# Merged runs of divided-array matmuls in a hybrid attention step: sample projections, scores and value products

## The chip, the cores and the metric

The kernel runs on one core of a Trainium2 chip. The metric is the device time of one execution in microseconds (us), taken over several runs; lower is better. The profile is of one further execution of the same program.

## The reference, cut to what matters

One layer of a streaming encoder is computed for two inputs at once: a prompt of 512 tokens and a "sample" of 32 new tokens (T = 32) that attends to caches. Three head groups work side by side: A (band attention, 6 heads), B (attention to keys picked by an indexer, 6 heads) and M (attention to 256 memory rows, 4 heads). All heads have 64 columns, and all arithmetic is float32.

```python
def _band_sample(q, k_new, v_new, k_cache, v_cache, table):      # group A, sample
    k = jnp.concatenate([k_cache, k_new], axis=1)                # 512 + 32 keys
    v = jnp.concatenate([v_cache, v_new], axis=1)
    return _attend(q, k, v, bias)                                # softmax(q k^T / 8 + bias) v
...
def _dsa_sample(q, k_new, v_new, qi, ki_new, wi, k_cache, v_cache, ki_cache):   # group B, sample
    k = jnp.concatenate([k_cache, k_new], axis=1)                # 1024 + 32 keys
    v = jnp.concatenate([v_cache, v_new], axis=1)
    return _gather_attend(q, k, v, _indexer_scores(qi, ki, wi), topk)
...
om = _attend(qm, cache_mem_k[l], cache_mem_v[l], None)           # group M, sample: 256 keys, none new
```

The sample's q, k and v come from the same input projection `rmsnorm(x) @ w_in` as the prompt's.

## The kernel before

**Layout.** TensorE does matmuls on 128 rows (the contraction) by 128 columns (the stationary operand's width). The weights `raw` arrive in chunks by DMA; each chunk is split into a high part `wh` (on ACT) and a low part `wl` (on POOL, a few on DVE), and the prompt's projections use three full-array matmuls for each product. These matmuls are the main stream that fills TensorE from start to end.

**Divided arrays.** The sample has only 32 rows, so its matmuls use a part of the array: the call names a `tile_position`, and several such matmuls run side by side. In the trace the form of a matmul begins with rows by columns: `128*128` is the whole array, `128*32` four column strips, `64*32` eight tiles, `128*64` two column halves, `32*64` a quarter of the rows by half of the columns. A float32 matmul has two records in the trace. A run is a stretch of consecutive matmuls of one division.

**Who orders the work.** There is no loop nest over the whole. Every piece of work is a Python generator, and the class `Line` (line 45) keeps one estimated clock for each engine while the program is written out. A generator yields the time at which it wants to go on; `Line.beside` (line 198) lets it go on when TensorE's estimated clock has got there, and between two such points the main stream goes on. So the order on every engine is fixed when the program is built, by the estimated costs of `Line.cost` (line 63), which know nothing of a change of division. On the chip every engine works through its own list in that order and waits where an operand is late. `Line.room(k)` (line 299, inside the kernel) waits until k of TensorE's 8 PSUM banks are free.

**What the change touches.**
- `w_sample` (line 456) makes the sample's rows of six projections in this order: `i`, `ka`, `va`, `kb`, `qb`, `vb`. Each has four weight chunks `raw` of two 128-row blocks; the eight blocks go to four column strips, twice four matmuls, in two halves (line 462): the first half as soon as two chunks are there, the second when the other two are. `met` (line 411) tells `w_load` (line 414) which chunks are used up; a chunk's successor four places on is loaded only then.
- `sample_rows` (line 471) adds up the four strips on ACT and DVE into a tile of 32 rows (`kaS`, `vaS`, `kbS`, `qbS`, `vbS`), and scales it; it is then in `news`, and `store_new` writes it out.
- `sample` (line 1127) is the sample's attention for one group. It takes the heads four at a time (then the last two): for chunks of 512 keys, `room()`, a bank, and one matmul for each head (lines 1155 to 1162), each chunk with a reduction on DVE; then the softmax; then transposes to `pt` (lines 1184 to 1200); then the value products, two heads at a time (line 1203), with a `yield line.soon()` between the pairs. The block of new keys has w = 32 rows, so its matmuls use `vv[0:w]` and `pt[0:w]`: 32 rows of the array.

Of the kernel before, what the change touches and what calls it, by code (L numbers as in the profile page):

```python
# [9 lines left out]
F32 = mybir.dt.float32  # L10
# [7 lines left out]
P = 128  # L18
S = 512
T = 32  # L20
# [249 lines left out]
def hybrid_step(ctx: ExitStack, tc: tile.TileContext, a: dict):  # L270
    ctx.enter_context(tc.manual_schedule())
    nc = tc.nc
    line = Line()
# [15 lines left out]
    def bank():  # L289
        b = min(free_banks, key=lambda b: pp.free(f"b{b}"))  # L290
        free_banks.remove(b)
        t = pp.tile([P, 512], F32, tag=f"b{b}", name="bank")
        held[t.tensor.name] = b
        return t
# [4 lines left out]
    def room(k=1):  # L299

        yield from line.wait(lambda: len(free_banks) >= k)
        while True:
            t = sorted(pp.free(f"b{b}") for b in free_banks)[k - 1] + 0.4
            if t <= line.now():
                return
            yield t
            yield from line.wait(lambda: len(free_banks) >= k)
# [60 lines left out]
    def store_new(dst, nm):  # L368
        def when():
            yield from line.wait(lambda: nm in news)  # L370
            yield line.at(news[nm])
            DMA.dma_start(dst, news[nm])

        line.spawn(when())

# [79 lines left out]

    def w_sample():
        for nm, i, n in parties:
            yield from line.wait(lambda: len(raws) > i + 1 and x_done[0] > 1)
            yield line.sure(xF[:, 0:4, :], raws[i + 1])
            yield from room()  # L460
            p = bank()
            for j in (0, 2):
                yield from line.wait(lambda: len(raws) > i + j + 1 and x_done[0] > j + 1)
                yield line.sure(raws[i + j], raws[i + j + 1], xF[:, 2 * j:2 * j + 4, :])
                for q in range(4):
                    PE.matmul(p[q * T:(q + 1) * T, 0:n], xF[:, 2 * j + q, :], raws[i + j + q // 2][:, q % 2, :],
                              start=(j == 0), stop=(j == 2), tile_position=(0, q * T))
                met.extend((i + j, i + j + 1))
            line.spawn(sample_rows(nm, n, p))

    def sample_rows(nm, n, p):
        yield line.at(p)
        if nm in ("kb", "vb"):
            yield from line.wait(lambda: 0 in over)
        out = (cp.tile([T, 384], F32, tag={"kb": "kaS", "vb": "vaS"}.get(nm, nm + "S"), name=nm + "S") if nm != "i"
               else ix.tile([T, n], F32, name="zS"))
        A.copy(out, p[0:T, 0:n])
        for q in range(1, 4):
            yield line.at(out) - 0.2
            V.tensor_tensor(out, p[q * T:(q + 1) * T, 0:n], out, op=ALU.add)  # L480
        give(p)
        yield from line.wait(lambda: NT in normed)
        yield max(line.at(rs[0:T, NT:NT + 1]), line.at(out) - 0.2)
        V.tensor_scalar(out, out, rs[0:T, NT:NT + 1], None, op0=ALU.mult)
        news[nm] = out
        if nm in ("kb", "qb"):
            rope(out.rearrange("p (h d) -> p h d", d=64), out, T, 6, 64, ctab["cos64S"], ctab["sin64S"], V)

# [638 lines left out]
    def sample(mix, nh, nb, kt, cv, qT, kn, vn, pts, zin):  # L1127

        kt0 = (0, 3, 6)[mix]
        nn = nb * P
        nk = nn + (T if kn is not None else 0)
        if kn is not None:
            yield line.sure(kn)
            yield from room()
            p = bank()
            for hp, k in enumerate(kt):
                PE.transpose(p[:, hp * T:(hp + 1) * T], kn[:, hp * P:(hp + 1) * P], ident[:T, :T])
            for hp, k in enumerate(kt):  # L1140
                either(k[:, nn:nk], p[:, hp * T:(hp + 1) * T])
            give(p)
        yield line.sure(qT, *kt)
        yield from room(3)
        o_ps = bank()
        for g0 in range(0, nh, 4):
            hs = list(range(g0, min(g0 + 4, nh)))
            rows = T * len(hs)
            z = zin(g0, rows)
            yield line.at(z)  # L1150
            if mix == 0:
                V.tensor_scalar(z[0:rows], z[0:rows], -1.0, None, op0=ALU.mult)
            st = cp.tile([P, 8], F32, tag="stS", name="stS", bufs=2)
            np_ = 0
            for k0 in range(0, nk, 512):
                n = min(512, nk - k0)
                yield from room()
                sc = bank()
                for j, h in enumerate(hs):
                    r = 64 * (h % 2)  # L1160
                    PE.matmul(sc[T * j:T * j + T, 0:n], qT[r:r + 64, h // 2, -T:], kt[h // 2][r:r + 64, k0:k0 + n], start=True, stop=True,
                              tile_position=(r, T * j))
                if mix != 2:
                    V.tensor_tensor_reduce(z[0:rows, k0:k0 + n], in0=sc[0:rows, 0:n], in1=z[0:rows, k0:k0 + n],
                                           scale=1.0, scalar=3e38, op0=ALU.add,
                                           op1=ALU.min, accum_out=st[0:rows, np_:np_ + 1])
                    src = z
                    give(sc)
                else:
                    V.tensor_reduce(st[0:rows, 0:1], sc[0:rows, 0:n], axis=AX.X, op=ALU.min)  # L1170
                    src = sc
                np_ += 1
            V.tensor_reduce(st[0:rows, 4:5], st[0:rows, 0:np_], axis=AX.X, op=ALU.min)
            yield line.at(st)
            A.activation(z[0:rows, 0:nk], src[0:rows, 0:nk], AF.Exp, scale=-1.0, bias=st[0:rows, 4:5],
                         accum_out=st[0:rows, 5:6])
            if mix == 2:
                give(sc)
            yield line.at(st)
            V.reciprocal(st[0:rows, 6:7], st[0:rows, 5:6])  # L1180
            V.tensor_scalar(z[0:rows, 0:nk], z[0:rows, 0:nk], st[0:rows, 6:7], None, op0=ALU.mult)
            yield line.sure(z)
            blocks = []
            for k0 in range(0, nk, 512):
                yield from room()
                bw = []
                p = bank()
                for i, b in enumerate(range(k0, min(k0 + 512, nk), P)):
                    w = min(P, nk - b)
                    PE.transpose(p[0:w, i * rows:(i + 1) * rows], z[0:rows, b:b + w], ident[0:rows, 0:rows])  # L1190
                    bw.append((b // P, i, w))
                pt = pts[k0 // 512]
                full = sum(1 for x in bw if x[2] == P)
                if full:
                    either(pt[:, 0:full * rows], p[:, 0:full * rows])
                else:
                    w = bw[-1][2]
                    either(pt[0:w, 0:rows], p[0:w, 0:rows])
                give(p)
                blocks += [(pt, b, i, w) for b, i, w in bw]  # L1200
            yield line.sure(*(x[0] for x in blocks))
            yield line.sure(*cv)
            for j0 in range(0, len(hs), 2):
                for pt, b, i, w in blocks:
                    for j in (j0, j0 + 1):
                        h = hs[j]
                        e = h % 2
                        vv = cv[b // 4][:, b % 4, h * 64:h * 64 + 64] if b < nb else vn[:, h * 64:h * 64 + 64]
                        PE.matmul(o_ps[64 * e:64 * e + 64, (h // 2) * T:(h // 2 + 1) * T], vv[0:w],
                                  pt[0:w, i * rows + T * j:i * rows + T * j + T], start=(b == 0),  # L1210
                                  stop=(b * P + w == nk), tile_position=(0, 64 * e))
                yield line.soon()
        yield from line.wait(lambda: mix in gated)
        m = nh // 2
        o = cp.tile([P, 3 * T], F32, tag="oSt", name="oSt")
        yield line.at(gates[mix], o_ps) - 0.2
        ov = o[:, 0:m * T].rearrange("p (m c) -> p m c", m=m)
        V.scalar_tensor_tensor(ov, o_ps[:, 0:m * T].rearrange("p (m c) -> p m c", m=m), 0.5, gates[mix][:, :, S:N],
                               op0=ALU.mult, op1=ALU.mult)
        give(o_ps)  # L1220
        rounded(oS[:, kt0:kt0 + m, 0:T], ov)
        tsub(V, oS[:, kt0:kt0 + m, T:2 * T], ov, f(oS)[:, kt0:kt0 + m, 0:T])
        over[mix] = True
# [481 lines left out]
```

## Time and profile before

| | us |
|---|---|
| median of 3 runs | 382.3 |
| lowest and highest | 382.24, 385.92 |
| the profiled execution's own time | 382.36 |
| its span in the profile | 380.6 |
| TensorE (PE) busy | 360.6 (95%) |
| VectorE (DVE) busy | 282.9 (74%) |
| ScalarE (ACT) busy | 221.4 (58%) |
| GpSimd (POOL) busy | 181.8 (48%) |

Busy time of PE counts overlapping matmuls once and takes in the pipeline's fill, so a busy PE may still lose time between two matmuls; the start times of successive matmuls show it. By line, nearly everything is at L240, the helper that records each call, so the rows are told apart by the names of the tiles.

### The profile page before, as it was taken

The numbers are of one execution on the slowest core, as the hardware profiler recorded it, in microseconds if no ns is written. First come the engines' busy times: TensorE is split into PE (matmuls) and PEld (weight loads), VectorE is DVE, ScalarE is ACT, GpSimd is POOL, SyncE is SP. The second block draws the span as 40 slices with busy tenths as digits, with TensorE's granted clock in tenths as the row PEclk, the third lists the DMA queues.
The fourth block names the chain that finished last, engine by engine and source line by source line (L and its number), as shares of the span: only waits on it lengthen the run. The fifth ranks groups of instructions, "written<-read, shape, count | busy, mean of one in ns | idle before, by whom it ended". The sixth has DMA issues, their size and how long they took to land.

```text
span 380.6 us, 7964 instructions
## 1 busy us (share of the span) xinstructions
PE 360.6 (95%) x2959; PEld 322.7 (85%) x2959; DVE 282.9 (74%) x732; ACT 221.4 (58%) x519; POOL 181.8 (48%) x196
## 2 busy tenths in 40 slices
PE   7999899999999999999999989699999999999992
PEld 6889798989988978888887877588999879799992
DVE  2671887699999998899899989784975667452553
ACT  4854756897546758679655145437873656211353
POOL 1778951475442653327454737445135315133542
PEclk9999989999999999999999999899999999999997
DMA  7996441266474151322121211412236942120005
GB/s 242 363 355 214 118 140 55 96 187 167 138 244 119 29 155 31 89 63 84 52 75 42 84 47 69 128 29 63 68 126 213 368 153 88 40 98 2 0 16 220
DMA packets 41478, 46.35 MB, mean 122 GB/s; under 512 B 5184, under 2 KB 36544, under 8 KB 41440
## 3 DMA queue, kind: packets, MB, share of 16 engines
q1 hardware_dynamic: 41440, 45.85, 38.0%
q8 instruction: 23, 0.38, 0.4%
q14 instruction: 15, 0.12, 0.1%
HBM read 39.67 MB, written 6.16 MB: 120 GB/s over the span
## 4 chain that ended last, share of the span: by engine, by line
PE 67%; DVE 21%; ACT 4%; issue 3%; POOL 2%; DMA 2%; SPq 1%; POOLq 0%; DVEq 0%; ACTq 0%
PE bank L240 67%; DVE ysel L240 5%; DVE m L240 2%; DVE rt L240 2%; DMA raw<-in_w_in_dram 2%; DVE qbS L240 2%; DVE rank L240 1%; POOL wl L240 1%; DVE st L240 1%; DVE kbS L240 1%; ACT sq L240 1%; ACT wh L240 1%; DVE junkS L240 1%; POOL ss L240 1%; ACT junkS L240 1%
## 5 line engine op out<-in xcount | busy, mean ns | idle before, releaser
L240 POOL TENSOR_TENSOR wl<-raw,wh 128x512 fp32r<-128x512 f32 (+2 forms) x68 | 107.4, 1587 | 112.7 <-ACT wh L240 109.4
L240 PE MATMUL bank<-wh,xTh 128*128 128x384 f32 (+1 forms) x192 | 67.6, 352 | 3.0 <-DVE kb L240 1.6
L240 ACT ACTIVATE wh<-raw 128x512 fp32r<-128x512 f32 (+2 forms) x70 | 49.6, 715 | 28.3 <-PE bank L240 12.7
L240 PE MATMUL bank<-wl,xTh 128*128 128x384 f32 (+1 forms) x192 | 64.3, 336 | 0.9 <-POOL wl L240 0.6
L240 PE MATMUL bank<-wh,xTl 128*128 128x384 f32 (+1 forms) x192 | 64.2, 334 | 0.0
L240 ACT ACTIVATE z<-z,st 128x256 f32<-128x256 f32 (+3 forms) x70 | 38.0, 557 | 27.0 <-DVE st L240 26.8
L240 PE MATMUL bank<-xTh,wh 128*128 128x272 f32 x208 | 46.4, 304 | 0.0
L240 PEld LDWEIGHTS bank<-wh,xTh 128*128 128x128 f32 x192 | 37.0, 193 | 9.4 <-issue 6.8
L240 PE MATMUL bank<-xTh,wl 128*128 128x272 f32 x208 | 43.0, 288 | 0.0
L240 PE MATMUL bank<-xTl,wh 128*128 128x272 f32 x208 | 42.9, 288 | 0.0
L240 PEld LDWEIGHTS bank<-wl,xTh 128*128 128x128 f32 x192 | 36.8, 192 | 1.4 <-POOL wl L240 0.8
L240 PEld LDWEIGHTS bank<-wh,xTl 128*128 128x128 f32 x192 | 37.0, 193 | 0.3 <-DVE xTl L240 0.3
L240 PEld LDWEIGHTS bank<-xTh,wh 128*128 128x128 f32 x208 | 32.7, 189 | 4.7 <-issue 3.3
L240 PEld LDWEIGHTS bank<-xTl,wh 128*128 128x128 f32 x208 | 32.6, 188 | 0.0
L240 PEld LDWEIGHTS bank<-xTh,wl 128*128 128x128 f32 x208 | 32.6, 189 | 0.0
L240 DVE MAX8 m<-ysel 128x8 f32<-128x256 f32 (+2 forms) x48 | 26.4, 549 | 0.1
L240 DVE MATCH_REPLACE8 ysel<-m,ysel 128x256 f32<-128x256 f32 (+2 forms) x48 | 26.1, 543 | 0.0
L240 PE MATMUL bank<-ident,z 128*128 128x128 f32 (+1 forms) x161 | 25.2, 275 | 0.6 <-ACT tg L240 0.6
L240 DVE TENSOR_TENSOR xr<-bank,xr 128x256 f32<-128x256 f32 (+1 forms) x24 | 12.3, 511 | 15.8 <-PE bank L240 15.8
L240 DVE SCALAR_TENSOR_TENSOR ysel<-r,wI,ysel 128x256 f32<-128x256 f32 (+2 forms) x21 | 18.9, 898 | 4.5 <-ACT r L240 3.7
L240 PEld LDWEIGHTS bank<-ident,z 128*128 128x128 f32 (+1 forms) x161 | 18.0, 140 | 4.5 <-issue 0.9
L240 ACT ACTIVATE junkS<-ysS,bi_neg 128x1056 int8<-128x1056 f32 x16 | 18.7, 1171 | 3.5 <-DVE bi_neg L240 3.5
(313 smaller groups left out, 887.2 us busy)
## 6 DMA issues: line engine op xcount, KB each, us to landing
raw<-in_w_in_dram SPq DMA_DIRECT2D x20, 384.0 KB, 3.4
raw<-in_w_in_dram SPq DMA_DIRECT2D x26, 256.0 KB, 3.0
raw<-in_w_out_dram SPq DMA_DIRECT2D x8, 384.0 KB, 3.0
nat<-in_x_prompt_dram SPq DMA_DIRECT2D x4, 512.0 KB, 8.4
raw<-in_w_mem_kv_dram SPq DMA_DIRECT2D x8, 256.0 KB, 2.8
xr<-in_x_prompt_dram SPq DMA_DIRECT2D x4, 512.0 KB, 7.0
out_dram<-xr SPq DMA_DIRECT2D x4, 512.0 KB, 2.6
xr<-in_x_t_dram SPq DMA_DIRECT2D x3, 544.0 KB, 6.0
```

Source lines behind the costliest of these rows:

```text
L240: return fn(*args, **kw)
```

## The change

The first half of a projection no longer starts ahead: `w_sample` waits for all four chunks and then issues the eight matmuls together. The value tiles of the new keys get 128 rows, 96 of them set to zero on POOL, and so does the transposed block of new keys in `pt`; the value products use all 128 rows. The score chunks of four heads get their banks together and their matmuls are issued together, the reductions after them. The `yield` between pairs of heads is gone.

```diff
@@ store_new
-            DMA.dma_start(dst, news[nm])
+            DMA.dma_start(dst, news[nm][0:T])
@@ w_sample
-            yield from line.wait(lambda: len(raws) > i + 1 and x_done[0] > 1)
-            yield line.sure(xF[:, 0:4, :], raws[i + 1])
+            yield from line.wait(lambda: len(raws) > i + 3 and x_done[0] > 3)
+            yield line.sure(xF, *raws[i:i + 4])
             yield from room()
             p = bank()
             for j in (0, 2):
-                yield from line.wait(lambda: len(raws) > i + j + 1 and x_done[0] > j + 1)
-                yield line.sure(raws[i + j], raws[i + j + 1], xF[:, 2 * j:2 * j + 4, :])
                 for q in range(4):
                     PE.matmul(p[q * T:(q + 1) * T, 0:n], xF[:, 2 * j + q, :], raws[i + j + q // 2][:, q % 2, :],
                               start=(j == 0), stop=(j == 2), tile_position=(0, q * T))
-                met.extend((i + j, i + j + 1))
+            met.extend(range(i, i + 4))
@@ sample_rows
-        out = (cp.tile([T, 384], F32, tag={"kb": "kaS", "vb": "vaS"}.get(nm, nm + "S"), name=nm + "S") if nm != "i"
-               else ix.tile([T, n], F32, name="zS"))
+        full = (cp.tile([P, 384], F32, tag={"kb": "kaS", "vb": "vaS"}.get(nm, nm + "S"), name=nm + "S") if nm != "i"
+                else ix.tile([P, n], F32, name="zS"))
+        out = full[0:T]
+        if nm[0] == "v":
+            G.memset(full[T:2 * T], 0.0)
+            G.memset(full[2 * T:P], 0.0)
...
-        news[nm] = out
+        news[nm] = full if nm[0] == "v" else out
@@ sample, scores
-            for k0 in range(0, nk, 512):
-                n = min(512, nk - k0)
-                yield from room()
-                sc = bank()
+            cuts = [(k0, min(512, nk - k0)) for k0 in range(0, nk, 512)]
+            yield from room(len(cuts))
+            scs = [bank() for _ in cuts]
+            for sc, (k0, n) in zip(scs, cuts):
                 for j, h in enumerate(hs):
                     r = 64 * (h % 2)
                     PE.matmul(sc[T * j:T * j + T, 0:n], ...)
+            for sc, (k0, n) in zip(scs, cuts):
                 if mix != 2:
                     V.tensor_tensor_reduce(...)
@@ sample, transposed block of the new keys
-                    w = bw[-1][2]
-                    either(pt[0:w, 0:rows], p[0:w, 0:rows])
+                    G.memset(pt[T:2 * T, 0:rows], 0.0)
+                    G.memset(pt[2 * T:P, 0:rows], 0.0)
+                    either(pt[0:T, 0:rows], p[0:T, 0:rows])
@@ sample, value products
-                        PE.matmul(o_ps[...], vv[0:w],
-                                  pt[0:w, i * rows + T * j:i * rows + T * j + T], start=(b == 0),
+                        PE.matmul(o_ps[...], vv,
+                                  pt[:, i * rows + T * j:i * rows + T * j + T], start=(b == 0),
                                   stop=(b * P + w == nk), tile_position=(0, 64 * e))
-                yield line.soon()
```

## Rows read from the trace of the kernel before

**Rows 1.** Busy time by stretch: start:end, length, engines, PE clock, DMA
```profile
135.00:182.00 47.00, 47.00 (x458) 39.90 (x455) 42.26 (x143) 34.61 (x92) 20.74 (x23) 1.00 0.29 85
187.00:244.00 57.00, 50.22 (x368) 43.29 (x365) 52.84 (x111) 25.58 (x66) 32.81 (x26) 0.99 0.26 76
243.20:246.70 3.50, 3.06 (x11) 3.06 (x12) 2.25 (x8) 3.47 (x12) 0.81 (x1) 0.51 0.01 2
244.00:367.00 123.00, 123.00 (x1100) 111.78 (x1100) 73.86 (x207) 61.85 (x153) 47.89 (x39) 0.99 0.29 97
```

**Rows 2.** The chain that ended last, in order: start us, length us, engine
```profile
111.40 74.47 PE bank L240 x694
```

**Rows 3.** DVE in order of time: start us, us; in brackets idle before, releaser
```profile
148.27 0.69 DVE L240 CUSTOM_DVE_ANT_0 z<-bank,nb 128x512 f32<-128x512 f32 x1 [0.92 <-PE bank L240]
...
156.06 0.42 DVE L240 COPY tmpA<-bank 128x256 f32<-128x256 f32 x1 [1.11 <-PE bank L240]
...
182.30 0.69 DVE L240 COPY pt<-bank 128x512 f32<-128x512 f32 x1 [0.82 <-PE bank L240]
```

**Rows 4.** PE in order of time around the sample's projection runs (`raw,xF`)
```profile
19.30 0.51 PE L240 MATMUL bank<-raw,xF 128*32 128x384 f32 x4
19.63 0.51 PE L240 MATMUL bank<-raw,xF 128*32 128x384 f32 x4
...
35.89 0.85 PE L240 MATMUL bank<-raw,xF 128*32 128x384 f32 x8
36.67 0.45 PE L240 MATMUL bank<-wh,xTh 128*128 128x384 f32 x1
36.96 0.34 PE L240 MATMUL bank<-wh,xTl 128*128 128x384 f32 x1
37.13 0.34 PE L240 MATMUL bank<-wl,xTh 128*128 128x384 f32 x1
```

**Rows 5.** DMA issues from 13.5 to 14.2 us: count, KB, us to landing
```profile
raw<-in_w_in_dram SPq DMA_DIRECT2D x1, 384.0 KB, 6.2
```

**Rows 6.** PE in order of time in value products, groups A and B
```profile
135.07 0.66 PE L240 MATMUL bank<-tmpA,cache 128*64 128x32 f32 x16
135.66 0.30 PE L240 MATMUL bank<-tmpA,vaS 32*64 32x32 f32 x4
135.90 0.52 PE L240 MATMUL bank<-xTh,wh 128*128 128x272 f32 x2
...
320.74 1.12 PE L240 MATMUL bank<-ptS,cache 128*64 128x32 f32 x32
```

**Rows 7.** PE in order of time around a score run of group A
```profile
142.97 0.41 PE L240 MATMUL bank<-xTl,wh 128*128 128x272 f32 x2
143.22 0.41 PE L240 MATMUL bank<-xTh,wl 128*128 128x272 f32 x2
143.56 0.25 PE L240 MATMUL bank<-keysA,queried 64*32 64x32 f32 x4
143.74 0.52 PE L240 MATMUL bank<-xTh,wh 128*128 128x272 f32 x2
144.10 0.29 PE L240 MATMUL bank<-xTl,wh 128*128 128x272 f32 x1
```

**Rows 8.** POOL groups by form: shape, count, busy us, mean ns
```profile
L240 POOL MEMSET nb<- 64x128 f32 x3 | 0.6, 198 | 8.1 <-DVE nb L240 8.1
```

**Rows 9.** POOL in order of time: start us, us
```profile
135.34 2.54 POOL L240 TENSOR_TENSOR wl<-raw,wh 128x512 fp32r<-128x512 f32 x2
...
235.11 5.84 POOL L240 TENSOR_TENSOR wl<-raw,wh 128x768 fp32r<-128x768 f32 x3
```

**Rows 10.** DVE groups by form: the same operation on two sample tiles
```profile
L240 DVE TENSOR_TENSOR qbS<-qbS,cos64S 32x384 f32<-32x384 f32 x1 | 2.1, 2062 | 0.0
...
L240 DVE TENSOR_TENSOR kbS<-kbS,cos64S 32x384 f32<-32x384 f32 x1 | 0.5, 547 | 0.0
```

**Rows 11.** PE in order of time: its longest wait
```profile
243.64 0.19 PE L240 MATMUL bank<-bf_ok,over 128*128 128x1 bf16 x1 [3.60 <-DVE o L240]
```

More of the change, by code (lines that the diff above doesn't have):

```diff
@@ L1208, in sample @@
                         vv = cv[b // 4][:, b % 4, h * 64:h * 64 + 64] if b < nb else vn[:, h * 64:h * 64 + 64]
-                        PE.matmul(o_ps[64 * e:64 * e + 64, (h // 2) * T:(h // 2 + 1) * T], vv[0:w],
-                                  pt[0:w, i * rows + T * j:i * rows + T * j + T], start=(b == 0),
+                        PE.matmul(o_ps[64 * e:64 * e + 64, (h // 2) * T:(h // 2 + 1) * T], vv,
+                                  pt[:, i * rows + T * j:i * rows + T * j + T], start=(b == 0),
                                   stop=(b * P + w == nk), tile_position=(0, 64 * e))
-                yield line.soon()
         yield from line.wait(lambda: mix in gated)
```

## The prediction, made before the result was seen

> **What bounds the kernel now.** I read the busy time by stretch first. Between 135 and 182 us TensorE (PE) is busy all 47.00 us, between 187 and 244 us only 50.22 of 57, and from 244 to 367 us again all of it [rows 1]. Busy does not mean dense, so the second look is at the chain of work that ended last: it lies on PE from 111.40 us for 74.47 us, that is to 185.9 [rows 2]. The reader is to see three regimes in these rows: PE sets the pace to about 186 us; from 187 to 244 us DVE does (52.84 of 57 us busy); after 244 us nothing holds PE up any more.
>
> The third look is at DVE in order of time. Ahead of 187 us it is nearly full too, so work saved on PE passes on only if DVE waits for PE somewhere. It does, at three places: 0.92 us at 148.27, 1.11 us at 156.06 and 0.82 us at 182.30 [rows 3]. The last is the start of the DVE-bound stretch, so what PE has gained by 182 us moves the whole of that stretch forward, as long as it is no more than these waits allow.
>
> [...]
>
> **The change part by part.**
>
> First the projection runs. In a float32 run a batch of four strips takes 0.33 us (19.30 to 19.63) [rows 4], so a half projection, two batches, has 0.65 us of work. The half at 35.89 takes 0.78 us up to the next full-array matmul, 0.13 too much. The first main matmul after it takes 0.29 us to the second (36.67 to 36.96), where 0.17 is the pace (36.96 to 37.13): another 0.12. Ahead of a run the gap grows by 0.09 (143.22 to 143.56 is 0.34 for two matmuls that take 0.25 a pair) [rows 7]. So a run costs 0.13 + 0.12 + 0.09 = 0.34 us beyond its work. Six projections had ten runs, since the second half of `i` and both halves of `ka` stood together. Five go. `va`'s (36 us) lies on PE's path: 0.34. `kb`'s (178 us) lies ahead of the wait at 182.30: 0.34. `qb`'s (200 us) and `vb`'s (230 us) lie inside the DVE-bound stretch: 0 each, PE only waits longer. `i`'s (13 us) counts 0 too: its work moves to 18.8 us, beside `ka`, and `ka`'s second half needs a chunk issued at 13.9 that takes 6.2 us to land [rows 5], so it is there at 20.1, while PE gets to that half two batches after 19.30, at 19.96. For these last three the bounds are 0 and 0.34 each.
>
> The moved halves keep their 0.65 us of work; the planner's clock puts as much of the main stream in their old places, so I cost the move at nothing. If PE had nothing else ready there, the half would be extra: at most 0.65 us, for `vb`, whose new place (247 us) is PE-bound.
>
> A chunk's successor is loaded later, since `met` now comes for all four at once: the wait put in delays it by up to the distance of the two halves, and what stands behind it are only the later chunks, for the loads are a generator of their own. The cover is the stock of split chunks, three of them (line 434): one of 384 columns feeds 4 x 6 matmuls of 0.17 us, 4 us, so 12 us of work stand against 6.2 us to land. Cost 0; with the cover gone it would cost what goes beyond 12 us.
>
> Next the new keys on all rows. Sixteen more records in a run of value products cost 1.12 - 0.66 = 0.46 us, 29 ns each, and a run of sixteen takes 0.59 us (135.07 to 135.66), so 0.12 us is fixed [rows 6]. The four records on 32 rows take 0.24 us (135.66 to 135.90); at 29 ns in the same run they take 0.12. That saves 0.12 us, six times: three in A, three in B.
>
> Then the value products in one run. The second run of a group of four heads goes: 0.09 ahead, 0.12 fixed, 0.11 behind (143.74 to 144.10 is 0.36 for a pair that takes 0.25 [rows 7]) = 0.32 us. Once in A (138 us), once in B (323 us), once in M (186 us). M's comes after 182.30 and falls into the DVE-bound stretch: 0 there, 0.32 at most.
>
> The scores in one run: A's late run of 32 columns costs 0.09 + 0.18 + 0.11 = 0.38 us [rows 7]; its four records inside the other run at 29 ns 0.12: saves 0.26. B's (309 us) has eight records and costs 0.39 by the same sum, less 0.23: 0.16. In exchange up to three banks are asked for at once. B's result is needed only by the last output projection (line 1635), so a wait for banks is hidden by the main stream; without that cover it costs what it lasts.
>
> What is added on POOL: two memsets of 384 columns each for `va` and `vb`, and two of 64 or 128 for each of four blocks of new keys. A memset of 128 columns took 198 ns [rows 8], so at most 0.6 us for one of 384: 2.4 + 1.6 = 4.0 us in all, as an upper bound. POOL is half idle, so I take 0 on the path. Behind a memset in POOL's list stands the next `wl`, which PE would wait for; the same stock of split chunks covers that. If that cover is gone: at most 1.2 us, once.
>
> The sum: 0.34 (`va`) + 0.34 (`kb`) + A's 3 x 0.12 + 0.32 + 0.26 = 0.94, + B's 3 x 0.12 + 0.32 + 0.16 = 0.84: 2.46 us. What is gained between 135 and 182 us is 1.28 us; by 148.27 it is 0.82, under that wait's 0.92, and the remaining 0.46 is under the 0.82 at 182.30, so DVE passes it on. The profiled execution took 382.36 us, the median is 382.3, so the two are the same: 382.36 - 2.46 = 379.9 us.
>
> [...]
>
> **The rivals.**
>
> First, DVE swallows what lies ahead of 187 us. For: DVE is busy 42.26 of 47 us there [rows 1]. Against: the three waits for PE. If small releases hold instead, `va`, `kb` and A's 0.94 are lost and B's 0.84 is left: 381.5 us. [...]
>
> Second, more than the sum. All parts count: 2.46 + 3 x 0.34 + 0.32 = 3.80, 378.6 us. And the stall at 243.64 need not come with a low clock again: 3.5 us at 0.51 did 1.7 us of full-speed work less [rows 1]; 376.9 us. For: the order is worked out anew from 13 us on. Against: nothing in the change aims at that stall.
>
> Third, slower: the new order puts more DVE work beside POOL. The list of every engine is remade, and in the DVE-bound stretch each sample-row operation that falls beside a `wl` costs 2.06 - 0.55 = 1.5 us [rows 10]. Now three in a row do, just ahead of the stall. `kb`'s rows have operations of the same size that are mostly clear of POOL. Two more of them beside POOL cancel the sum; four more give +3.6 us: 386.0 us. The same toss can free those that collide now: 4.5 us less, 375.4 us. For: memsets and moved runs shift the plan by more than such an operation lasts. Against: no wait is added there.
>
> Fourth, a new wait. Value products now wait for memsets. In A, POOL had two `wl` from 135.34 to 137.88 [rows 9], beside the run at 135.07. If the memset falls behind them, the block of new keys, last in its run, waits some 2.4 us, and 382.3 us results; it is slower than before if both of A's runs wait.
>
> **How the numbers follow.** A difference of 1%, 3.8 us, is about what a measurement of this kernel can tell from no change. Chances: the sum as worked out (378.5 to 381) 0.38; swallowed, held up by memsets or waiting for them (381 to 382.4) 0.14; more than the sum, with the clock or freed operations (under 378.5) 0.28; slower by the new order or wait 0.20, of it 0.12 beyond 386.1. Faster by over 1% is the third case, 0.28; slower 0.12; the rest, 0.60, within 1%. The range 376 to 385 us leaves out about one in ten at the top and less at the bottom; the likeliest case's own is 378.5 to 381.
>
> **What would show it.** Right: projection runs of 16 records with nothing between the halves, `i` and `ka` perhaps in one; no `32*64` form with `vaS` or `vbS`; one run of value products for each group of heads, 29 ns a record; the DVE wait at 182 starting about 1.3 us earlier; PE busy throughout from the end of the DVE stretch, with about 0.8 us less in it. Wrong: PE waiting for a memset, the operations on `kbS` or `qbS` at 2 us in other numbers than now, another length of the stall near 243 us, or a low clock at another place. Those would move the time by more than the runs do.

## The result, and the profile after

| | before | after |
|---|---|---|
| median, us | 383.0 (382.24 to 385.92, 4 runs) | 369.48 (369.0 to 369.77, 4 runs) |
| the profiled execution, us | 382.36 | 369.7 |
| its span, us | 380.6 | 367.9 |
| PE busy, us | 360.6 | 355.6 |
| DVE busy, us | 282.9 | 282.4 |
| ACT busy, us | 221.4 | 223.0 |
| POOL busy, us | 181.8 | 176.2 |

The ratio is 0.969, with a 95% interval from 0.964 to 0.973: 3.1% faster. The forecast was 379.9 us, with a range from 376 to 385; the time lies 6.5 us under the range.

The span fell by 12.7 us. PE's busy time gives only 5.0 of them, so the larger part, 7.7 us, is time in which PE stood still (12.7 us before, 5.0 after). The list of PE's waits says where it went; its longest lines are shown. The first fence is the kernel before, the second the changed kernel (engine and line, what was waited for, us in total, times, longest):

```profile
PE bank L240 <- DVE o L240: 3.6, 1, 3.6
PE bank L240 <- DVE kb L240: 1.6, 1, 1.6
PE bank L240 <- POOL nhalf L240: 1.4, 1, 1.4
PE bank L240 <- DVE ka L240: 1.2, 1, 1.2
PE bank L240 <- POOL wl L240: 1.0, 2, 0.6
```

```profile
PE bank L240 <- POOL nhalf L240: 1.4, 1, 1.4
PE bank L240 <- DVE o L240: 1.3, 1, 1.3
PE bank L240 <- DVE stk L240: 0.7, 2, 0.4
```

The reader is to see that the long waits are gone: the one for `o` [rows 11] is 1.3 instead of 3.6 us, and the one for `kb` isn't in the list any more. The change touches neither of these two operations. It does touch the projection `qb`, and three operations on its rows `qbS` stand ahead of that `o` in DVE's list before; afterwards they come at 229.8 us, behind PE's last long wait. Whether that is the reason has to be tested.

The stretches that [rows 1] showed look like this afterwards (start:end, length, busy time and instructions of PE, PE's weight loads, DVE, ACT, POOL, then the granted clock, DMA share, GB/s):

```profile
135.00:182.00 47.00, 47.00 (x458) 41.03 (x458) 45.08 (x143) 34.15 (x88) 21.61 (x24) 1.00 0.24 69
187.00:244.00 57.00, 55.07 (x371) 48.28 (x370) 53.27 (x116) 29.27 (x74) 31.06 (x26) 0.97 0.25 73
225.60:229.00 3.40, 3.40 (x13) 2.96 (x13) 3.16 (x8) 1.56 (x3) 1.64 (x1) 0.50 0.98 308
229.00:355.00 126.00, 126.00 (x1156) 114.56 (x1157) 79.22 (x217) 65.58 (x167) 47.37 (x45) 1.00 0.29 97
```

In the second row DVE is as busy as it was before (53.27 against 52.84 us), and yet PE lost 1.9 us there instead of 6.8. The two rows hold the same length of time and not the same work. Still, a busy DVE did not set the pace by its amount of work; what counted was which of its operations PE waited for.

The chain that ended last (start us, length us, what) says when PE was held up for the last time. The first fence is before, the second after:

```profile
243.64 123.19 PE bank L240 x1095
```

```profile
133.39 61.64 PE bank L240 x567
224.17 129.98 PE bank L240 x1164
```

After the last long wait the chain stays on PE until about 14 us before the end, in both kernels. Before, that began at 243.64 us with 123.19 us of work left; now it begins at 224.17 with 129.98 left. 19.5 us earlier, less 6.8 us more work, is the 12.7 us. The upper line of the second fence says that PE now keeps the chain to 195.0 us instead of 185.9 [rows 2]: the stretch in which the chain is mostly on other engines is 29 us long (195.0 to 224.2) instead of 58 (185.9 to 243.6).

The runs themselves became what the change says. PE in order of time, a projection pair and the value products of group A (start us, us, instruction):

```profile
18.42 2.49 PE L240 MATMUL bank<-raw,xF 128*32 128x296 f32 x32
20.84 0.40 PE L240 MATMUL bank<-wh,xTh 128*128 128x296 f32 x1
...
129.71 0.66 PE L240 MATMUL bank<-tmpA,cache 128*64 128x32 f32 x16
130.19 0.29 PE L240 MATMUL bank<-tmpA,vaS 128*64 128x32 f32 x4
130.31 0.64 PE L240 MATMUL bank<-tmpA,cache 128*64 128x32 f32 x16
130.78 0.29 PE L240 MATMUL bank<-tmpA,vaS 128*64 128x32 f32 x4
131.00 1.11 PE L240 MATMUL bank<-keysA,queried 64*32 64x512 f32 x8
```

`i` and `ka` stand in one run of 32 records, and no `32*64` form is left. Counted over the whole trace, stretches of one division fell from 156 to 126; not all of it is the joining, since another order of the kernel before has 151.

So there were two theories. **Order**: the joined runs give about what the sum of the prediction says, and the rest comes from the order in which the planner writes all the other work, which it makes anew whenever anything changes. **Structure**: joining the runs itself frees DVE and PE from those waits, or leads the planner to orders without them.

### The profile page after: what moved, and what is told of

It reads as the page before. It is cut to its first block, busy times and chain, and to the rows that moved or that the text cites. A ratio compares the mean times of both kernels' runs of the same rounds, so it can differ in the third digit from the quotient of the medians.

```text
span 367.9 us, 7969 instructions
## 1 busy us (share of the span) xinstructions
PE 355.6 (97%) x2959; PEld 321.6 (87%) x2959; DVE 282.4 (77%) x731; ACT 223.0 (61%) x524; POOL 176.2 (48%) x202
## 4 chain that ended last, share of the span: by engine, by line
PE 77%; DVE 11%; ACT 3%; POOL 3%; issue 2%; DMA 2%; SPq 1%; POOLq 0%; ACTq 0%; DVEq 0%
PE bank L240 77%; DMA raw<-in_w_in_dram 2%; DVE rt L240 1%; POOL wl L240 1%; DVE rank L240 1%; DVE KSs L240 1%; ACT sq L240 1%; DVE ysel L240 1%; DVE kb L240 1%; POOL ss L240 1%; DVE kbS L240 1%; DVE m L240 1%; SPq L240 1%; DVE bf_m L240 1%; POOL kb L240 1%
## 5 line engine op out<-in xcount | busy, mean ns | idle before, releaser
L240 POOL TENSOR_TENSOR wl<-raw,wh 128x512 fp32r<-128x512 f32 (+2 forms) x68 | 105.1, 1553 | 95.6 <-ACT wh L240 91.8
L240 ACT ACTIVATE z<-z,st 128x256 f32<-128x256 f32 (+3 forms) x76 | 40.6, 549 | 35.1 <-DVE st L240 35.0
```

What stands on the lines that cost most here:

```text
L240: return fn(*args, **kw)
```

## Experiments

Three figures are worked out from each trace, to compare orders: the sum of PE's waits; the length of the stretches at a low granted clock, which was 0.50 to 0.51 in them (within 243.2 to 246.7 us before [rows 1], 225.6 to 229.0 in the changed kernel) and 1.00 beside them, those at the start and in the last 15 us left out; and the rest, the span less the waits and less half of those stretches. The rest is about what PE needs when nothing holds it up and the granted clock is 1.00. It is good to about 1 us, since a wait and a slow stretch can overlap. It can't say whether PE's saving reaches the end: what PE saves and then waits longer lowers the rest and raises the waits. Ratios are those of the timed runs against runs of the kernel before on the same chip.

### The joined runs on the old order

In `kept_order` the planner books each operation at its old place, but the matmuls of a projection, and the value products of four heads, are held back and issued together. The memsets are issued without being booked. The other instructions keep the order of the kernel before on every engine. The scores keep their old runs, since their banks can't be held longer without moving other work.

```diff
                 for q in range(4):
-                    PE.matmul(p[...], xF[...], raws[...], ...)
+                    line.op("PE", "matmul", ...)
+                    held_back.append(...)
+                if j == 2 or nm not in ("i", "va", "kb", "qb", "vb"):
+                    for a_, kw in held_back:
+                        nc.tensor.matmul(*a_, **kw)
```

`line.op` books a matmul, `nc.tensor.matmul` issues it. The value products are treated in the same way, on 128 rows.

> Projections and value products run as in the changed kernel (eight matmuls of a projection together, value products of four heads together on 128 rows, with the memsets), but the planner is told of each operation at its old place, so that every other instruction keeps the order of the kernel before on every engine. The scores keep their old runs. Theory 'order' (the runs give about what the sum says, the other 9 us come from the re-made order): 382.4 minus 2 to 3.3 us, that is 379 to 380.5 us, and PE's wait of 3.6 us near 243 us and the second half-clock window beside it stay. Rival 'structure' (the joined runs themselves free DVE and PE, the order of the rest is secondary): 371 to 375 us, and PE's waits fall from 12.7 us to 6 or less. Rival 'DVE swallows' of the prediction: 381 to 382 us.

Measured: 379.13 us, ratio 0.991 (0.988 to 0.995), that is 3.3 us less (2.1 to 4.4). The long wait is where it was, of the same length, 3 us earlier:

```profile
240.71 0.19 PE L240 MATMUL bank<-bf_ok,over 128*128 128x1 bf16 x1 [3.60 <-DVE o L240]
```

The profiled execution took 380.65 us. In its trace the rest fell by 2.3 us (364.5 to 362.2), PE's waits rose by 0.5 (12.7 to 13.2), and the slow stretches are as long in all as before (6.8 us).

What follows: the joined runs alone give about 3.3 us, and they don't touch the stall. Structure falls for these two parts, as far as it means the runs themselves.

### Each part alone, the order made anew

> The kernel before with the projections' part alone: eight matmuls in one run, and the order of everything else made anew. Theory 'order': the runs saved are worth 0.7 to 1.7 us, the new order adds several us of either sign: anything from 372 to 386 us, and what the time goes with is the sum of PE's waits and the half-clock windows, not the runs. Rival 'structure, in the projections': 370 to 373 us, nearly the whole gain of 12.7 us. Rival 'structure, elsewhere': 380.5 to 381.7 us.

> The kernel before with the scores' part alone: banks together, matmuls of a group of four heads in one run, reductions after them. Theory 'order': runs saved worth 0.2 to 0.4 us, with a shift of several us of either sign from the order made anew. Rival 'structure, in the scores': 370 to 374 us. Rival 'structure, elsewhere': 381.8 to 382.3 us.

> The kernel before with the value products' part alone: 128 rows for the new keys with the memsets, and no point between the pairs of heads at which the main stream goes on. Theory 'order': runs saved worth 1.4 us (six times 0.12, two or three times 0.32), with a shift of several us of either sign. Rival 'structure, in the values': 370 to 374 us. Rival 'structure, elsewhere': 380.8 to 381.2 us.

Each is the kernel before with one part of the diff shown above: the hunk of `w_sample`; the hunk of the scores; the hunks of `store_new`, `sample_rows`, the transposed block and the value products. Measured: projections 382.06 us, ratio 1.000 (0.997 to 1.002); scores 380.83 us, 0.996 (0.993 to 1.000); values 381.82 us, 1.000 (0.996 to 1.003). No part brings the gain: by the ratios the three come to 1.6 us together, of 12.7. So structure falls for each part by itself; the theory of order allowed nearly any time here and is not tested by it. The projections show how a saving vanishes. Their rest fell by 1.9 us (364.5 to 362.6), but the new order has a wait that the old one did not have, and slow stretches of 10.2 us instead of 6.8. The wait, from PE in order of time, and the stretch beside it with the granted clock at 0.51:

```profile
214.89 0.58 PE L240 MATMUL bank<-k,q 64*128 64x256 f32 x1 [5.47 <-DVE kl L240]
...
213.70:220.60 6.90, 5.71 (x32) 3.73 (x33) 6.76 (x16) 0.83 (x2) 2.02 (x2) 0.51 0.00 0
```

### Other orders of the kernel before

No line that makes an operation is changed, only one constant of the planner: its margin for a wait on another engine, the 1.0 us that it adds for operands that must surely be there (the expectations call it a factor), a term in its cost of a matmul, its lag. An order takes in one thing more than the places: by its estimated clocks the planner also picks the engine of some operations, copies above all. At the margin 0.31, for example, five copies into `pt` and three scalings of `z` went from DVE to ACT, and one operation on `kb` from POOL to DVE.

```diff
-        self.margin = 0.3
+        self.margin = 0.31
...
-SURE = 1.0
+SURE = 1.02
...
-            return 0.003 + n
+            return 0.0035 + n
...
-LAG = 0.2
+LAG = 0.21
```

Each of the four is a kernel of its own.

> The kernel before, not one operation changed; the planner's small margin for a cross-engine wait is 0.31 instead of 0.30, so that the order on the engines comes out a little differently. Theory 'order': the time moves by several us for nothing, in the direction of PE's waits; 372 to 386 us. Rival 'structure': within 1 us of 382.4 us.

> As the run before it, with another constant of the planner: the factor by which it holds back where an operand must surely be there is 1.02 instead of 1.00. Theory 'order': 372 to 386 us, with another time than the run with the margin. Rival 'structure': within 1 us of 382.4 us.

> The kernel before, not one operation changed; in the planner's cost of an operation one constant is 0.0035 instead of 0.0030 us. A third order of the old kernel beside the margin's (375.8) and the factor's (381.4). If most old orders have a stall with a half-clock window between 190 and 250 us: 379 to 384 us, with such a stall; if the order of the kernel before was an unlucky one: 374 to 377 us.

> The kernel before, not one operation changed, the planner's lag 0.21 instead of 0.20: a fifth order of the old kernel. Both theories: one more draw from 375 to 383 us; with the other four it gives the mean from which the joined runs' share is taken.

Measured: 375.75, 381.38, 379.84 and 382.28 us (the ratios are in the table below). One order of the same work is 1.5% faster (ratio 0.985, 0.979 to 0.992; its four runs took 373.8 to 378.7 us) than the kernel before; three are within 0.4%. The choice of engines alone is not the reason: at 1.02 the planner made the same moves and one more, and gained nothing. The stall with a low clock that was expected for the cost of 0.0035 came without the low clock. In the faster order the wait for `o` is gone and the one for `kb` is 0.2 us, and PE's chain to the end begins at 230.45 us:

```profile
PE bank L240 <- POOL nhalf L240: 1.3, 1, 1.3
PE bank L240 <- ACT z L240: 1.0, 2, 0.8
PE bank L240 <- POOL wl L240: 0.9, 1, 0.9
...
230.45 127.97 PE bank L240 x1139
```

What follows: a gain in waits of 6.6 us, half of the 12.7, is to be had without the change. The order of the kernel before was not an outlier: three of the four others are like it.

### Other orders of the changed kernel

> The changed kernel, not one operation changed, the planner's margin 0.31 instead of 0.30. Theory 'order' (the changed kernel's order is one lucky draw): 368 to 380 us, more likely longer than 369.5 than shorter. Rival 'structure': within 1 us of 369.5 us.

> The changed kernel, not one operation changed, the planner's factor for operands that must surely be there 1.02 instead of 1.00. If 369.5 us is one lucky order among many: 373 to 380 us. If joined runs lead the planner to orders without the stall near 225 to 245 us: 368 to 371.5 us again.

> The changed kernel, not one operation changed, the planner's margin 0.33 instead of 0.30 (0.31 left the changed kernel's order as it was, so that run was a repeat). Theory 'one lucky order': 372 to 381 us, about 3 us under the mean of the old kernel's orders (382, 381.4, 379.8, 375.8; mean 379.8), with a wait of PE of 2 us or more or a half-clock window between 190 and 260 us. Theory 'joined runs lead to better orders': 368 to 372 us.

> The changed kernel, not one operation changed, the planner's factor for operands that must surely be there 0.98 instead of 1.00. Theory 'one lucky order': 372 to 381 us. Theory 'joined runs lead to better orders': 368 to 372 us, and then the 379.8 us of the factor 1.02 is the outlier.

> The changed kernel, not one operation changed, the constant in the planner's cost of an operation 0.0025 instead of 0.0030 us. Theory 'one lucky order': 372 to 381 us. Theory 'joined runs lead to better orders': 368 to 372 us.

The constants are those of the runs before, at 0.31 and 0.33 (margin), 1.02 and 0.98 (added time), 0.0025 (cost). The margin of 0.31 left every engine's list as it was, so `after_margin` is a repeat of the changed kernel and no other order: 369.65 us against 369.48. The other four gave 379.84, 375.0, 375.91 and 376.91 us. The slowest has the joined runs and is only 0.4% faster than the kernel before (ratio 0.996, 0.993 to 0.998). Its longest waits of PE:

```profile
PE bank L240 <- DVE kl L240: 2.8, 1, 2.8
PE bank L240 <- DVE qb L240: 2.2, 1, 2.2
```

All orders together, with the three figures of each trace in us:

| order | ratio to before | span | PE's waits | low clock | rest |
|---|---|---|---|---|---|
| **old runs:** before | 1 | 380.6 | 12.7 | 6.8 | 364.5 |
| margin 0.31 | 0.985 | 372.2 | 6.1 | 0 | 366.0 |
| added time 1.02 | 1.002 | 379.1 | 12.4 | 3.4 | 364.9 |
| cost 0.0035 | 0.996 | 378.3 | 11.9 | 0 | 366.4 |
| lag 0.21 | 1.002 | 381.3 | 12.1 | 6.8 | 365.8 |
| **joined runs:** after | 0.969 | 367.9 | 5.0 | 3.4 | 361.1 |
| added time 1.02 | 0.996 | 378.4 | 14.3 | 3.4 | 362.4 |
| margin 0.33 | 0.982 | 373.7 | 10.5 | 6.8 | 359.8 |
| added time 0.98 | 0.984 | 373.4 | 7.8 | 6.8 | 362.2 |
| cost 0.0025 | 0.987 | 376.4 | 10.4 | 10.2 | 360.9 |

Two things are to be read here. The rest separates the two groups without overlap: 364.5 to 366.4 with the old runs (mean 365.5), 359.8 to 362.4 with the joined ones (mean 361.3). That is 4.2 us less for the joined runs, as a mean over the orders. And the waits and the slow stretches scatter in both groups, from 5 to 14 us and from 0 to 10 us, with no gain on average: the waits and half of the slow stretches come to 12.7 us in the mean of either group. So nothing here says that joined runs lead to better orders. The means of the ratios are 0.997 and 0.983: the groups are 1.4% apart, 5.2 us. With scatters of 0.7% and 1.0% over five orders each, the standard error of that difference is 0.5%, 2 us. With the two kernels of the comparison left out, the other four and four orders are 0.9% apart, 3.5 us.

So, by these means and with that error, the 3.1% consist of 1.4% that go with the joined runs, 0.3% by which the order of the kernel before was slower than the mean of its kind, and 1.5% by which that of the changed kernel is faster than the mean of its kind. The theory of one lucky order holds: the other four orders of the changed kernel are 1.3 to 2.8% slower than it. None of the orders tried is faster than the changed kernel.

### The joined runs on the faster old order

The edits of `kept_order` on the order of the margin 0.31.

> The kernel before with the planner's margin at 0.31 (375.8 us), and on that order, kept on every engine, projections and value products in their joined runs as in the changed kernel. If order and runs add up: 375.8 less the 3.3 us that the same edit gave on the old order, 372 to 373 us. If the runs saved are worth more where nothing waits for DVE (the stalls no longer take them back): 370 to 371.5 us. If the gain of the joined runs is lost on this order: 375 us or more.

Measured: 374.08 us, ratio 0.982 (0.977 to 0.986), against 0.985 for that order without the joined runs: 1.4 us less, which the intervals don't separate from nothing, nor from 3.3. In the traces the rest fell from 366.0 to 362.6 us, and the waits rose from 6.1 to 8.0, one for `z` from 0.6 to 1.6 us among them:

```profile
PE bank L240 <- ACT z L240: 1.6, 3, 0.8
PE bank L240 <- DVE z L240: 1.6, 1, 1.6
```

A slow stretch of 3.4 us came in besides, and the two spans are the same (372.2 and 372.3 us). The time is in none of the three ranges expected. In the trace PE's saving is whole and is given back, as waits and as the slow stretch; how much of it is left in the time stays open.

### What makes the stall of 3.6 us

Here the lists of PE and DVE are those of the kernel before. The three `wl` on POOL of [rows 9] (from 235.11 us) are copies on ACT instead, still booked on POOL, so that POOL is idle beside DVE's operations on `qbS`. The low part of three weight chunks is thereby left out.

```diff
-            tsub(V if i in WV else G, wl, raw, f(wh))
+            if i in (48, 49, 50):
+                line.op("POOL", "tensor_tensor", ...)
+                nc.scalar.activation(wl, raw, AF.Copy)
+            else:
+                tsub(V if i in WV else G, wl, raw, f(wh))
```

> The kernel before, each list in the old order, but the three `wl` that POOL runs from 235.11 us, beside DVE's three operations on the sample rows `qbS`, are copies on ACT instead; the low part of these three weight chunks is left out of the computation. Theory 'the collision makes the stall' (three DVE operations of 2.0 us fall to 0.4 to 0.55, 4.5 us, so that PE's wait of 3.6 us for `o` near 243 us goes, and the half-clock window behind it): 376.5 to 378.8 us, the half-clock window gone. Theory 'DVE is late there anyway' (the wait moves to another operation): 380.5 to 382.5 us.

Measured: 378.98 us, ratio 0.995 (0.992 to 0.999), 1.8 us less. DVE in the kernel before, in order of time:

```profile
235.16 1.98 DVE L240 TENSOR_SCALAR qbS<-qbS,rs 32x384 f32<-32x384 f32 x1
237.25 2.01 DVE L240 TENSOR_TENSOR rt<-qbS,sin64S 32x384 f32<-32x384 f32 x1
239.29 2.06 DVE L240 TENSOR_TENSOR qbS<-qbS,cos64S 32x384 f32<-32x384 f32 x1
...
243.17 0.41 DVE L240 SCALAR_TENSOR_TENSOR o<-bank,gate 128x256 f32<-128x256 f32 x1
```

DVE, then PE, in this run:

```profile
236.52 0.41 DVE L240 TENSOR_SCALAR qbS<-qbS,rs 32x384 f32<-32x384 f32 x1
237.03 0.55 DVE L240 TENSOR_TENSOR rt<-qbS,sin64S 32x384 f32<-32x384 f32 x1
237.61 0.55 DVE L240 TENSOR_TENSOR qbS<-qbS,cos64S 32x384 f32<-32x384 f32 x1
...
241.22 0.42 DVE L240 SCALAR_TENSOR_TENSOR o<-bank,gate 128x256 f32<-128x256 f32 x1 [0.83 <-PE bank L240]
...
236.45 0.38 PE L240 MATMUL bank<-k,q 64*128 64x256 f32 x1 [1.27 <-ACT pt L240]
237.66 0.54 PE L240 MATMUL bank<-k,q 64*128 64x256 f32 x1 [0.83 <-ACT pt L240]
...
244.39 0.18 PE L240 MATMUL bank<-bf_ok,over 128*128 128x1 bf16 x1
```

DVE's three operations take 1.5 us instead of 6.1, and PE's wait of 3.60 us in front of `bf_ok,over` is gone. PE itself comes later to that matmul here, but `o` is done at 241.64, 2.75 us ahead of it, although DVE had waited 0.83 us for PE just before `o`. The collision made that stall: this is shown. The time is 0.2 us above what that theory expected, and the low clock did not go: PE waits 2.1 us for `pt`, ahead of which ACT's copies now stand, and the granted clock is low from 237.7 for 3.4 us: the pairs of `k,q`, `k,ql` and `kl,q` start 0.21 to 0.22 us apart there (238.00 to 238.65), against 0.11 to 0.12 at a clock of 1.00 in the changed kernel (224.40 to 224.75). Measured against the kernel before at the same matmuls of the main stream, the trace gains 1.9 us between 221 and 264 us.

It does not follow that freeing these operations makes an order fast. With the added time of 1.02 and with the cost of 0.0035 in the kernel before, the three take 0.40, 0.55 and 0.55 us as well, and those orders are at most 0.4% faster: PE waits elsewhere, 4.7 us for `kb` at 227.6 us in the one, 2.0 for `o` and 2.3 for `kb` in the other.

### 32 rows again, in the changed order

> The changed kernel, with the value products of the new keys on 32 rows again; the memsets stay, and so does every instruction's place on every engine. What it costs is the price of a division of its own inside a run, six times, with nothing else changed. The sum's step (0.12 us each, more now that the pairs stand in one run and alternate with it: ten changes of division instead of six) gives 370.2 to 370.8 us. If DVE or POOL set the time where these runs stand: 369.5 us, no difference.

```diff
-                        PE.matmul(o_ps[...], vv,
-                                  pt[:, ...], ...)
+                        PE.matmul(o_ps[...], vv[0:w],
+                                  pt[0:w, ...], ...)
```

Measured: 370.22 us against 369.48, ratios 0.970 (0.966 to 0.974) and 0.969 (0.964 to 0.973), which don't separate them. The lists are the same, so the traces can be laid side by side, matmul by matmul. Group B's first four heads, first on 32 rows, then on 128 (the last line of each fence is only the start of the run that follows):

```profile
310.94 1.07 PE L240 MATMUL bank<-ptS,cache 128*64 128x32 f32 x32
311.94 0.30 PE L240 MATMUL bank<-keysB,vbS 32*64 32x32 f32 x4
312.18 1.12 PE L240 MATMUL bank<-ptS,cache 128*64 128x32 f32 x32
313.23 0.30 PE L240 MATMUL bank<-keysB,vbS 32*64 32x32 f32 x4
313.47 1.48 PE L240 MATMUL bank<-keysB,qbS 64*32 64x512 f32 x6
```

```profile
309.62 1.07 PE L240 MATMUL bank<-ptS,cache 128*64 128x32 f32 x32
310.53 0.29 PE L240 MATMUL bank<-keysB,vbS 128*64 128x32 f32 x4
310.64 1.10 PE L240 MATMUL bank<-ptS,cache 128*64 128x32 f32 x32
311.58 0.29 PE L240 MATMUL bank<-keysB,vbS 128*64 128x32 f32 x4
311.79 0.62 PE L240 MATMUL bank<-keysB,qbS 64*32 64x512 f32 x2
```

2.53 us (310.94 to 313.47) against 2.17: three more changes of division, 0.12 us each, which is the term of the prediction. Behind B's six heads, with four more changes, the main stream is 0.46 us later, and stays so to the end. Group A's first four heads cost the same 0.36 us more, and nothing of it arrives: the main stream is 1.21 us later after them, as it was 1.20 us later ahead of them from waits near the start. There the changed kernel waits 0.32 us for `stS` on DVE, and the other doesn't.

## Why the prediction was wrong, point by point

**The step that failed** is that the sum was set against an order held fixed, and the change of order was put at nothing in it. Each term was worked out at the old places, and the change of order stood as a rival: DVE operations that fall beside POOL or get clear of it, from 4.5 us less to 3.6 us more, with a small chance at either end. That rival named the right agent, and the operations: the three on `qbS` did get clear (0.40, 0.55 and 0.55 us at 229.8 us in the changed kernel), and the prediction's signs of being wrong came, in those operations, in the stall of 1.3 instead of 3.6 us and in a low clock at another place. But the order acts through every wait between engines, not through that collision alone: two orders of the kernel before have these operations clear and gain at most 0.4%. And it acts always: orders of the same work lie 6.5 us apart with the old runs and 10.2 us apart with the joined ones, by their ratios. Against a saving of 4 us, this scatter should have set the range. Of the five orders of the changed kernel, 376 to 385 us holds only two by their times. That the forecast missed by as much as it did is the draw, and so luck: 5.6 us of it by the means above.

**What bounds the kernel.** PE sets the pace to 186 us and again from 244: right for the kernel before. That DVE sets it between, because it is busy 52.84 of 57 us [rows 1], was read too strongly: DVE is equally busy in that window of the changed kernel, and PE loses 4.9 us less.

**The terms of the sum.** Where a run can be read by itself, they are right. The joined value run of A takes 1.29 us (129.71 to 131.00) for what were two of 0.83 [rows 6] and, by the prediction's own figures, 0.20 around the second, 0.57 saved; the prediction had 2 x 0.12 + 0.32 = 0.56. The traces of the single parts agree for the projections, whose rest is 1.9 us under the kernel before's, where five runs of 0.34 are 1.7. For the value products they don't show it: the rest is 0.6 us higher, where the sum has 1.36 less. The orders of the old runs scatter by 1.9 us in this figure, so it settles no single term. The memsets cost nothing: 0.14 to 0.21 us for the small ones, 0.41 to 0.42 for those of 384 columns (the bound was 0.6), and no wait of PE names one. The moved halves cost nothing that shows either.

**The zeros.** `i`, `qb`, `vb` and M were put at nothing in the sum of 2.46 us because PE would only wait longer there; with them all parts come to 3.80. Projections and value products on the kept order gave 3.3 us (2.1 to 4.4), without the scores, for which the sum has 3.38 if all count and 2.04 with the zeros. That speaks for counting them, but the interval ends just above 2.04. The rest over all orders fell by 4.2 us, so PE saves about the whole 3.80; whether all of it reaches the end is not shown, since the rest leaves out the waits. A DVE wait does swallow a part now and then, as in A's first group above.

**The rivals.** DVE swallows the saving: it does so in places, and not as a whole. A new wait on memsets: no. Slower by new order: not in this order, but the mechanism is real, and it cost 4.6 us in the order of added time 1.02 against the mean of its kind. More than the sum: this came, though for 5.6 us of it the reason is the draw and not "all parts" and the clock. The clock gave back about what the rival said, but not surely: of two stretches at a granted clock of 0.51, from 48.6 to 52.0 us and beside the stall [rows 1], one is left, at 0.50 from 225.6 us, behind the wait of 1.3 us, and the second execution of the same lists (`after_margin`) has none, at the same time, since it waited 1.4 us longer elsewhere.

**Memsets beside DVE.** The chances name a time held up by memsets; no run shows memsets that hold up DVE. In the changed kernel two DVE operations ran beside the two memsets of `vaS`. POOL, then DVE, in order of time in the changed kernel:

```profile
45.34 0.87 POOL L240 MEMSET vaS<- 32x384 f32 x2
...
45.95 0.21 DVE L240 TENSOR_TENSOR kst<-rotS,kst 32x64 fp32r<-32x64 f32 x1
46.09 0.47 DVE L240 SCALAR_TENSOR_TENSOR mTl<-mr,g_mem,mTh 128x256 fp32r<-128x256 f32 x1
```

The first lies wholly beside the memsets, the second begins beside them; they take 0.21 and 0.47 us. In the kernel before the same two took 1.06 and 2.05 us, at 48.9 and 44.9 us, each beside a `wl` (from 48.10 for 1.83 us and from 44.53 for 2.15).

What stays open is why this one order is so good. Its waits are few, and which decision of the planner leads there, a place in a list or the choice of an engine, was not traced; the runs only show that small changes of its constants lead elsewhere.

## What to carry to other kernels

Where a planner orders the work by estimates, a change's time is its own saving plus a draw from the orders that it may lead to. Measure that draw first, by changing a constant that leaves the work as it is, and compare groups of orders, or keep the order and change the runs alone; one timing of each kernel can't tell a saving of 1% from a draw of 2%. A busy engine was the bound here only where another waited for it: DVE was busy 52.84 and 53.27 of 57 us, and PE lost 6.8 and 1.9. Price a wait by what PE loses, not by the busy share.

## What the runs showed of the hardware

Three DVE operations on 32x384 float32 took 1.98, 2.01 and 2.06 us beside a POOL `wl`, and 0.41, 0.55 and 0.55 us when that POOL work went to ACT, with everything else on DVE in place. The first of them is the multiplication by a column, which has one tile as input. Two other DVE operations took 0.21 and 0.47 us beside memsets on POOL, and 1.06 and 2.05 us beside a `wl`. A change of division cost 0.12 us, read from two traces that differ in the rows of the new keys' blocks alone (2.53 against 2.17 us, three changes more).
